# Four look-up chunks compared beside the gate build, first dot products ahead of the pipeline, spill rows moved forward

## The chip, the cores and the metric

The kernel runs on one core of a Trainium2 chip. A core has a matrix engine (TensorE, PE in the rows), a vector engine (VectorE, DVE), a scalar engine (ScalarE, ACT), a general one (GpSimd, POOL) and one that only issues transfers (SyncE, SP). Each takes its instructions in order, and they wait for one another by semaphores. DMA queues of SP, ACT and POOL move data between HBM and the on-chip memory. The metric is the device time of one execution in microseconds, the median of several runs.

## The reference

One encoder layer on 256 tokens of width 2048: a retention and a recurrent branch, cross attention, and a PEER layer, followed by a last norm. Only PEER matters here:

```python
sub_scores = jnp.einsum('thcd,hckd->thck', q, sub_keys)
vals, ids = lax.top_k(sub_scores, PEER_TOPK)
...
top_sc, pos = lax.top_k(cand, PEER_TOPK)
eid = (i1 * PEER_N_KEYS + i2).reshape(t, PEER_HEADS * PEER_TOPK)
gate = jax.nn.softmax(top_sc, axis=-1)
...
u = u_tab[eb]
act = jax.nn.gelu(jnp.einsum('td,tkd->tk', xb, u))
out = jnp.einsum('tk,tkd->td', gb * act, v_tab[eb])
```

Every token chooses 128 of 16384 experts (8 heads, 16 each). An expert is a row of a table `u` and a row of a table `v`, 2048 wide.

## The kernel before

Some experts are chosen by many tokens, others by few. The kernel works the frequent ones densely, as blocks of 128 experts against all 256 tokens, and the others by token: the row of each chosen expert is fetched and multiplied with the token.

*The gate build* (`gbuild`, lines 1105 to 1167; about 1019 to 1165 us) makes, four tokens at a time, the gate of every expert and token (products `G`, L1146) and counts how often each of 88 groups of experts is chosen (`cnt`, L1149). ACT copies `G` into two staging buffers `gs`, the halves `ga` and `gb` (L1152, L1153), and after each of eight groups writes them to memory (L1156 to L1159). `gb` takes turns in three buffers of the tag "ms".

*Dense U blocks* (`u_chunk`, L156) run on PE from before the gate build until 1253 us: five chunks of eight columns, two weight blocks per column, 80 in all. Each block is loaded into `raw` by SP, cast to `hi` by ACT (L135), its rest `lo` taken by DVE (L136), and multiplied as 16 products with `hi` and 8 with `lo`.

*The choice* (`side`, that is `choose` and then `compact`) is woven into these blocks: a list of work is emitted a step at a time between products (`wv.pump`), and a scheduler then orders each engine. `choose` finds the 32 most frequent of the groups and builds `words`, a bit table (L960 to L972; `pow` is a small constant it loads). `compact` looks up, for each of two tiles of 128 tokens, whether each chosen expert is among them: `look_up` takes four chunks per tile, eight in all. A chunk is a 1 MB broadcast load of expert groups (`at_load`, L990, issued by POOL, from `i1d`), a compare in two halves on DVE (L997), 32 small products on PE (L1001, `look<-words`), and two DVE operations on the result (L1005, L1007). Chunks 0, 1, 2, 6 and 7 use h[1] and two pieces `gx`, and 3, 4 and 5 use `at3` to `at5`, three "ms" buffers which the gate build has used last. Then DVE picks the rows to fetch (MAX and MATCH_REPLACE, L935 and L936) and makes their indices; what does not fit into 38 rows per token goes into *spill rows*, whose token (`spti`) and expert (`spi`) are worked out at the end of `compact`.

*The D phase* (1253 to 1495 us) works 32 columns of experts fetched by row (`row<-in_Us_dram`, L1231): PE transposes them (L1372), ACT and DVE split them into `hi` (L1381) and `lo` (L1400), PE multiplies (L145, L147). *V steps* follow until 1903 us with `v`. Both are written out by hand (`run`): each engine keeps the order in which the code emits. Between the steps the generator `chosen` emits, as often as a step's rate allows, one operation for each fetched row: a *dot* with the token (DVE, L1462), a *spill* (a dot of a fetched row with a fetched token, L1542), and in the V steps an *axpy* that adds the row of `v` to the result `hh` (L1470). Rows are fetched by POOL (`fetch`, L1455) into a ring of buffers; a buffer returns when the row behind it was used. Three rows are fetched ahead (`ahead`). Each spill op takes two ring buffers, for the row of `u` and for the token's row of `hn`; they stand behind dot 19 of tile 0 and dot 10 of tile 1. h[0] holds tile 0's tokens (`h`), then tile 1's.

*The end* (`v_final`, from 1903 us) multiplies the last blocks (L1636) on PE while DVE adds the last 12 rows (`closing`) and ACT and DVE form the norm.

## Time and profile before

| | us |
|---|---|
| runs before, median (lowest to highest) of 3 | 1977.03 (1976.32 to 1978.99) |
| profiled execution | 1978.82 |
| its span | 1977.0 |
| look-ups: 1157.5 to 1253.4 | 95.9 |
| D phase: 1253 to 1495 | 242 |
| V steps: 1495 to 1903 | 408 |
| end: 1903 to 1977 | 74 |

The span is the time from the first to the last instruction in one profiled execution; all rows are from it. A row of a timeline has the start, the duration (of the whole group where xN stands), the engine, the line, the operation, the tiles and, in brackets, how long the engine stood idle just before and what ended that wait.

### The profile page before, as it was taken

To read this page: it belongs to the slowest core of one execution; us is meant where nothing else is said; L and a number is where in the kernel's file an instruction comes from. 1 tells how busy PE (TensorE), PEld (TensorE's weight loads), DVE (VectorE), ACT (ScalarE), POOL (GpSimd) and SP (SyncE) were. 2 spreads that over 40 slices of the span, in tenths; PEclk is the share of its full clock that TensorE was granted. 3 is DMA by queue.
4 is the path that set the end of the run, shared out by engine and by line. 5 is a ranking of instruction groups with operands and counts; after the bars stand their busy time and mean duration, and the time that the engine had idled before them with its cause. 6 is when DMAs were issued, how large, how long until landed. Compare 5 with 4: busy or idle time off the path is not lost.

```text
span 1977.0 us, 28501 instructions
## 1 busy us (share of the span) xinstructions
PE 1896.1 (96%) x10644; PEld 1589.4 (80%) x10644; DVE 1500.9 (76%) x2304; ACT 851.6 (43%) x1324; POOL 517.7 (26%) x370
## 2 busy tenths in 40 slices
PE   9999999999999999999999887999989989999997
PEld 8888888888889888899899877988978668656563
DVE  6867968654566656899986667798879889687857
ACT  6566444544455554554456542333334343121111
POOL 0200010000000000000025421355443578477723
PEclk9999999999999999999999988999989999999999
DMA  8775755566664456755557888699898989999993
GB/s 297 260 224 170 208 195 182 154 185 195 185 185 156 149 167 217 251 176 164 186 179 142 166 258 277 235 395 362 321 383 318 383 315 399 379 387 372 421 411 125
DMA packets 203391, 500.97 MB, mean 253 GB/s; under 512 B 106777, under 2 KB 113049, under 8 KB 174873
## 3 DMA queue, kind: packets, MB, share of 16 engines
q1 hardware_dynamic: 72576, 256.33, 39.7%
q0 software_dynamic: 36096, 227.24, 29.5%
q10 hardware_dynamic: 94576, 15.54, 4.8%
q8 instruction: 84, 1.38, 0.3%
q14 instruction: 59, 0.48, 0.1%
HBM read 504.29 MB, written 21.30 MB: 266 GB/s over the span
## 4 chain that ended last, share of the span: by engine, by line
PE 56%; DMA 17%; DVE 14%; issue 9%; POOL 2%; ACT 2%; ACTq 0%; SPq 0%; POOLq 0%; DVEq 0%
PE wb L145 8%; PE xc L198 7%; PE xc L199 7%; PE xc L201 7%; DMA at<-in_Us_dram,idx 6%; PE acc L1213 6%; PE wb L147 4%; PE U L156 4%; DVE lo L136 4%; DMA gt<-gs 3%; DMA at<-in_Vs_dram,idx 2%; DMA kept<-in_V_dram 2%; PE G L1146 2%; PE acc L1194 2%; PE acc L1191 2%
## 5 line engine op out<-in xcount | busy, mean ns | idle before, releaser
L136 DVE TENSOR_TENSOR lo<-raw,hi 128x1024 fp32r<-128x1024 f32 x364 | 448.9, 1235 | 217.3 <-PE xc L201 125.7
L135 ACT CAST hi<-raw 128x1024 fp32r<-128x1024 f32 x364 | 382.1, 1053 | 352.4 <-PE xc L199 173.4
L156 PE MATMUL U<-xn,hi 128*128 128x256 f32 x1280 | 179.9, 292 | 3.8 <-ACT hi L135 3.8
L156 PEld LDWEIGHTS U<-xn,hi 128*128 128x128 f32 x1280 | 167.0, 199 | 4.7 <-ACT hi L135 4.7
L1462 DVE SCALAR_TENSOR_TENSOR junk<-at,h 128x2048 bf16<-128x2048 f32 x64 | 146.2, 2284 | 9.1 <-DMA at<-in_Us_dram,idx 8.9
L1470 DVE SCALAR_TENSOR_TENSOR hh<-at,coef,hh 128x2048 f32<-128x2048 f32 x46 | 108.0, 2348 | 47.3 <-DMA at<-in_Vs_dram,idx 46.7
L145 PE MATMUL U<-xn,hi 128*128 128x512 f32 x512 | 140.2, 407 | 0.0
L794 POOL DMA_DIRECT2D hn<-h x2 | 1.1, 565 | 510.4 <-DVE h L792 510.4
L1383 ACT CAST hi<-kept 128x1024 fp32r<-128x1024 f32 x52 | 53.6, 1051 | 186.9 <-DMA kept<-in_Vs_dram,dyn 127.0
L1455 POOL DMA_INDIRECT at<-in_Us_dram,idx x72 | 86.3, 1199 | 143.4 <-DVE junk L1462 114.4
L145 PE MATMUL wb<-hT,hi 128*128 128x512 f32 x448 | 116.9, 396 | 0.7 <-ACT hi L135 0.7
L1213 PE MATMUL acc<-kept,kept 128*128 128x512 f32 x256 | 110.2, 592 | 0.0
L1133 POOL TENSOR_TENSOR kept<-kept 128x512 f32<-128x512 bf16 x64 | 72.0, 1133 | 130.1 <-DVE kept L1132 90.2
L145 PEld LDWEIGHTS U<-xn,hi 128*128 128x128 f32 x512 | 92.9, 192 | 15.4
L156 PE MATMUL U<-xn,lo 128*128 128x256 f32 x640 | 96.0, 295 | 5.9 <-DVE lo L136 5.5
L1213 PEld LDWEIGHTS acc<-kept,kept 128*128 128x128 f32 x256 | 48.6, 190 | 60.4 <-issue 60.3
L156 PEld LDWEIGHTS U<-xn,lo 128*128 128x128 f32 x640 | 86.5, 201 | 9.2 <-DVE lo L136 8.9
L145 PEld LDWEIGHTS wb<-hT,hi 128*128 128x128 f32 x448 | 80.6, 189 | 14.8 <-ACT hi L135 0.9
L1400 DVE TENSOR_TENSOR lo<-uT,hi 128x512 fp32r<-128x512 f32 x128 | 81.8, 682 | 11.6 <-ACT hi L1381 8.7
L145 PE MATMUL wb<-xT,hi 128*128 128x512 f32 x352 | 90.1, 398 | 0.0
L1132 DVE TENSOR_TENSOR kept<-kept,kept 128x512 bf16<-128x512 bf16 x128 | 63.1, 543 | 32.8 <-PE cnt L1149 23.3
L1455 POOL DMA_INDIRECT at<-in_Vs_dram,idx x46 | 76.0, 1653 | 41.0 <-issue 18.6
(502 smaller groups left out, 4399.3 us busy)
## 6 DMA issues: line engine op xcount, KB each, us to landing
raw<-in_U_dram SPq DMA_DIRECT2D x80, 512.0 KB
raw<-in_w_qkv_dram SPq DMA_DIRECT2D x48, 512.0 KB
raw<-in_w_xyg_dram SPq DMA_DIRECT2D x44, 512.0 KB
raw<-in_V_dram SPq DMA_DIRECT2D x44, 512.0 KB
raw<-in_w_xk_dram SPq DMA_DIRECT2D x32, 512.0 KB
raw<-in_w_xv_dram SPq DMA_DIRECT2D x32, 512.0 KB
raw<-in_w_out_dram SPq DMA_DIRECT2D x32, 512.0 KB
raw<-in_w_xq_dram SPq DMA_DIRECT2D x32, 512.0 KB
```

The costliest lines, as they stand in the source:

```text
L135: A.copy(hi, raw)
L136: V.tensor_tensor(lo, raw, hi.bitcast(F32), op=ALU.subtract)
L145: PE.matmul(pt, hi[:, ks], xt[:, kb, :], start=(kb == 0), stop=(kb == KB - 1))
L156: PE.matmul(pt[:, :T], (lo if part == 2 else hi)[:, k * P:(k + 1) * P], x, start=(part == 0 and kb == 0), stop=(part == 2 and kb == KB - 1))
L198: PE.matmul(pt, xh, hi[:, w], start=(n == 0 and k == 0), stop=False)
L199: PE.matmul(pt, xl, hi[:, w], start=False, stop=False)
L201: PE.matmul(pt, xh, lo[:, w], start=False, stop=(n == 7 and k == 1))
L1213: PE.matmul(acc[dc][tt], av[:, c, tt * P:(tt + 1) * P], row[:, dc * 512:(dc + 1) * 512], start=False, stop=False)
L1400: V.tensor_tensor(los[t][:, s], pts[t][n], his[t][:, s].bitcast(F32), op=ALU.subtract)
L1455: G.indirect_dma_start(dst, None, src, bass.IndirectOffsetOnAxis(ap=ix, axis=0), bounds_check=n - 1, oob_is_err=False)
L1462: V.scalar_tensor_tensor(junk, gat, 1.0, h[0] if rows is None else rows, op0=ALU.mult, op1=ALU.mult, accum_out=coef[tt][:, k:k + 1])
L1470: V.scalar_tensor_tensor(hh[tt], gat, coef[tt][:, k:k + 1], hh[tt], op0=ALU.mult, op1=ALU.add)
```

## The change

The places of the eight look-up chunks are set before the gate build (`places`): h[1], a piece `kept8`, an "ms" buffer `at`, h[0], two pieces of `gx`, then h[1] and `kept8` again. Chunks 0 to 3 are loaded there, and their compares are emitted inside `gbuild` at its steps 20, 30, 40 and 50. The two remaining "ms" buffers hold `gb` in turns. Only chunks 4 to 7 are loaded behind the gate build, 6 and 7 when look-ups 0 and 1 are done. h[0] is reloaded from `hn` by SP behind look-up 3, and the next `hn` load stands behind look-up 5 instead of 3. The first three rows are fetched into `at` and the two `gb` buffers, which then serve as the ring. A loop ahead of the last chunk's gelu emits work until the look-ups are done, since `kept8` holds that chunk's result. The spill tokens are fetched into two `gx` pieces before the D phase, the spill ops stand behind dots 8 and 14 of tile 0 and take one ring buffer each, and three dots are emitted before the hand-written part begins, so that all later dots and axpys come three earlier.

```diff
-SPILL_AT = (19, 10)
+SPILL_AT = (8, 14)
+LOOK_AT = (20, 30, 40, 50)
+EARLY = 3
...
         gates = gbuild()
-        at_load(0)
+        tr["t"] = rp.tile([P, P + 1], F32, tag="cand", name="tri")
+        nc.sync.dma_start(tr["t"], a["tri"])
+        places()
+        for i in range(4):
+            at_load(i)
...
+    def compare(i):
+        at = at_of(i)
+        for n in range(0, 32, 16):
+            V.tensor_scalar(at[:, n:n + 16], at[:, n:n + 16], tr["t"][:, P:], None, op0=ALU.is_equal)
+            yield 0.7
+
+    def places():
+        gbs.extend(slot("ms", [P, P // 2, GT], "gs") for _ in range(2))
+        held = held_in[NCH - 1]
+        ats.extend((h[1], held, slot("ms", [P, D], "at"), h[0], gx["a"], gx["d"], h[1], held))
...
     def look_up(tt):
         for c in range(4):
             at = at_of(4 * tt + c)
-            for n in range(0, 32, 16):
-                V.tensor_scalar(at[:, n:n + 16], at[:, n:n + 16], tr["t"][:, P:], None, op0=ALU.is_equal)
-                yield 0.7
+            if tt:
+                yield from compare(4 * tt + c)
...
-            if 4 * tt + c + len(ats) < 4 * TT:
-                at_load(4 * tt + c + len(ats))
+            if not tt and c < 2:
+                at_load(6 + c)
+            if 4 * tt + c == 3:
+                nc.sync.dma_start(h[0], hn[:P, :])
...
-            if tt and c < 2:
-                ahead.append(fetch(ats[4 + c], a["Us"], NS, idx[0][:, 1 + c:2 + c]))
-            if tt == 0 and c == 3:
+            if 4 * tt + c == 5:
                 nc.sync.dma_start(held_in[NCH + NDY - 1], hn[P:2 * P, :])
...
             if tt == 0:
-                ahead.append(fetch(ats[3], a["Us"], NS, idx[0][:, 0:1]))
+                for n, b in enumerate([ats[2]] + [g.rearrange("p a b -> p (a b)") for g in gbs]):
+                    ahead.append(fetch(b, a["Us"], NS, idx[0][:, n:n + 1]))
...
     def side():
-        ats.extend((gx["a"], gx["d"]))
-        ats.extend(slot("ms", [P, D], f"at{i}") for i in (3, 4, 5))
-        for i in range(1, 6):
+        for i in range(4, 6):
             at_load(i)
...
         for n in range(T // 4 + 1):
+            if n in LOOK_AT:
+                yield from compare(LOOK_AT.index(n))
...
-                    ga, gb = (slot(tag, [P, P // 2, GT], "gs") for tag in ("qs", "ms"))
+                    ga, gb = slot("qs", [P, P // 2, GT], "gs"), gbs[m // (GT // 4) % 2]
...
+            while i == NCH - 1 and not c and "looked" not in done:
+                wv.pump(1.0)
             A.activation(acts[i][:, c, :], pt[:, :T], AF.Gelu_apprx_tanh)
...
     def chosen():
+        spl["x"] = [fetch(gx["bc"[b]], hn, T, spl["ti"][:, b:b + 1]) for b in range(TT)]
...
-                if k == SPILL_AT[tt]:
-                    ops.append(("spill", tt, 0, [(a["Us"], NS, spl["i"][:, tt:tt + 1]), (hn, T, spl["ti"][:, tt:tt + 1])]))
+                if tt == 0 and k in SPILL_AT:
+                    b = SPILL_AT.index(k)
+                    ops.append(("spill", b, 0, [(a["Us"], NS, spl["i"][:, b:b + 1])]))
...
-    wv.add(chosen())
+    row_ops = chosen()
+    for _ in range(EARLY):
+        next(row_ops)
+    wv.add(row_ops)
```

The scheduler moves what is emitted. The compares of chunks 0 to 3 end up on DVE ahead of the whole gate build, where chunk 0's stood before. On PE, all four look-ups of the first tile now follow one another, and behind look-up 5 stand the products of blocks 64 and 65 with `hi` and `lo`, half of look-up 6, the products of blocks 66, 67 and 68 with `hi` alone, the rest of look-up 6 and half of 7, and only then those of 66 with `lo`. On SP, before: the load of `pow`, one `raw`, one `hn`, then 12 `raw`; now: `pow`, one `raw`, two `hn`, then 13 `raw`, each with the waits of its buffer.

Three places on DVE follow. Line numbers of the changed kernel are its own (there L138 is the `lo` of L136, L1023 and L1025 the two steps on a look-up of L1005 and L1007, L1030 to L1034 the steps of L1014 to L1018, L941 the pick of L935, L1481 the dot of L1462, L1419 the `lo` of L1400). The first place is just ahead of the picks of the first token tile; before:

```order
L136 TENSOR_TENSOR lo_11426<-raw_11423,hi_11425 128x1024
L1014 CAST kept1_7764<-kept1_7764 128x128
L1005 TENSOR_TENSOR kept1_7764<-look_11343,kept2_7765 128x352
L1015 TENSOR_TENSOR kept1_7764<-kept1_7764,kept2_7765 128x128
L136 TENSOR_TENSOR lo_11494<-raw_11491,hi_11493 128x1024
L1016 TENSOR_SCALAR kept1_7764<-kept1_7764 128x128
L136 TENSOR_TENSOR lo_11574<-raw_11571,hi_11573 128x1024
L1018 TENSOR_TENSOR key_8575<-key_8575,kept1_7764 128x128
L1018 TENSOR_TENSOR work_8576<-work_8576,kept1_7764 128x128
L935 MAX sel_11195<-key_8575 128x8
```

and in the changed kernel (h1 holds chunk 6 there):

```order
L1025 TENSOR_REDUCE kept1_7764<-kept1_7764 128x32
L997 TENSOR_SCALAR h1_4236<-h1_4236,tri_9497 128x2048
L1030 CAST kept1_7764<-kept1_7764 128x128
L138 TENSOR_TENSOR lo_11314<-raw_11311,hi_11313 128x1024
L1031 TENSOR_TENSOR kept1_7764<-kept1_7764,kept2_7765 128x128
L1023 TENSOR_TENSOR kept1_7764<-look_11341,kept2_7765 128x352
L1032 TENSOR_SCALAR kept1_7764<-kept1_7764 128x128
L138 TENSOR_TENSOR lo_11419<-raw_11416,hi_11418 128x1024
L1034 TENSOR_TENSOR key_8575<-key_8575,kept1_7764 128x128
L1034 TENSOR_TENSOR work_8576<-work_8576,kept1_7764 128x128
L941 MAX sel_11187<-key_8575 128x8
```

Three `lo` blocks stood ahead of the picks, now there are two, and the first half of chunk 6's compare stands ahead of both. The second place is behind these picks, where the two tiles' work meets; before (kept0 holds chunk 7):

```order
L950 SCALAR_TENSOR_TENSOR sel2_11196<-sel_11195,sel2_11196 128x56
L1005 TENSOR_TENSOR kept1_7764<-look_11455,kept2_7765 128x352
L997 TENSOR_SCALAR kept0_7763<-kept0_7763,tri_10949 128x2048
L1007 TENSOR_REDUCE kept1_7764<-kept1_7764 128x32
L136 TENSOR_TENSOR lo_11624<-raw_11621,hi_11623 128x1024
L1005 TENSOR_TENSOR kept1_7764<-look_11522,kept2_7765 128x352
L136 TENSOR_TENSOR lo_11682<-raw_11679,hi_11681 128x1024
L1007 TENSOR_REDUCE kept1_7764<-kept1_7764 128x32
L136 TENSOR_TENSOR lo_11736<-raw_11733,hi_11735 128x1024
L1014 CAST kept1_7764<-kept1_7764 128x128
L136 TENSOR_TENSOR lo_11801<-raw_11798,hi_11800 128x1024
L1015 TENSOR_TENSOR kept1_7764<-kept1_7764,kept2_7765 128x128
```

and in the changed kernel (kept8 holds chunk 7):

```order
L956 SCALAR_TENSOR_TENSOR sel2_11188<-sel_11187,sel2_11188 128x56
L997 TENSOR_SCALAR kept8_7771<-kept8_7771,tri_9497 128x2048
L138 TENSOR_TENSOR lo_11487<-raw_11484,hi_11486 128x1024
L997 TENSOR_SCALAR kept8_7771<-kept8_7771,tri_9497 128x2048
L138 TENSOR_TENSOR lo_11567<-raw_11564,hi_11566 128x1024
L1023 TENSOR_TENSOR kept1_7764<-look_11515,kept2_7765 128x352
L138 TENSOR_TENSOR lo_11617<-raw_11614,hi_11616 128x1024
L1025 TENSOR_REDUCE kept1_7764<-kept1_7764 128x32
L138 TENSOR_TENSOR lo_11675<-raw_11672,hi_11674 128x1024
L1030 CAST kept1_7764<-kept1_7764 128x128
L138 TENSOR_TENSOR lo_11729<-raw_11726,hi_11728 128x1024
L1031 TENSOR_TENSOR kept1_7764<-kept1_7764,kept2_7765 128x128
```

Four `lo` blocks are seen there before and five now; ahead of this piece the compare of at5 is gone, and the blocks that follow are lower in number by two. The third place is the start of the D phase; before:

```order
L136 TENSOR_TENSOR lo_12079<-raw_12076,hi_12078 128x1024
L1083 TENSOR_SCALAR spt_11724<-spt_11724 128x1
L1088 SCALAR_TENSOR_TENSOR j1_11787,w1_11784<-iota_79,w1_11784,ls_11779 128x18
L1090 CAST spi_11726<-w1_11784 128x1
L1091 SCALAR_TENSOR_TENSOR j1_11787,spg_11727<-iota_79,w1_11784,ls_11779 128x18
L1400 TENSOR_TENSOR lo_12184<-uT_12135,hi_12175 128x512
L1400 TENSOR_TENSOR lo_12184<-uT_12136,hi_12175 128x512
L1400 TENSOR_TENSOR lo_12187<-uT_12145,hi_12178 128x512
L1400 TENSOR_TENSOR lo_12187<-uT_12146,hi_12178 128x512
L1400 TENSOR_TENSOR lo_12203<-uT_12155,hi_12181 128x512
L1400 TENSOR_TENSOR lo_12203<-uT_12156,hi_12181 128x512
L1462 SCALAR_TENSOR_TENSOR junk_12117,coef_12226<-at3_10951,h0_4235 128x2048
```

and in the changed kernel:

```order
L1481 SCALAR_TENSOR_TENSOR junk_12110,coef_12117<-at_9501,h0_4235 128x2048
L138 TENSOR_TENSOR lo_12042<-raw_12039,hi_12041 128x1024
L138 TENSOR_TENSOR lo_12072<-raw_12069,hi_12071 128x1024
L1481 SCALAR_TENSOR_TENSOR junk_12110,coef_12117<-gs_9499,h0_4235 128x2048
L1481 SCALAR_TENSOR_TENSOR junk_12110,coef_12117<-gs_9500,h0_4235 128x2048
L1419 TENSOR_TENSOR lo_12194<-uT_12145,hi_12185 128x512
L1419 TENSOR_TENSOR lo_12194<-uT_12146,hi_12185 128x512
L1419 TENSOR_TENSOR lo_12197<-uT_12155,hi_12188 128x512
L1419 TENSOR_TENSOR lo_12197<-uT_12156,hi_12188 128x512
L1419 TENSOR_TENSOR lo_12213<-uT_12165,hi_12191 128x512
L1419 TENSOR_TENSOR lo_12213<-uT_12166,hi_12191 128x512
L1481 SCALAR_TENSOR_TENSOR junk_12110,coef_12117<-at_9501,h0_4235 128x2048
```

One dot now stands ahead of the last two `lo` blocks of U and two more ahead of the first `lo` of the D phase, where before there was none until its sixth row.

More of the change, by code (lines that the diff above doesn't have):

```diff
@@ L981, in chosen_rows @@
         yield 0.8
-    ats = []
+    ats, gbs = [], []
     def at_of(i):
-        return ats[i % len(ats)].bitcast(BF16).rearrange("p (s t) -> p s t", t=P)
+        return ats[i].bitcast(BF16).rearrange("p (s t) -> p s t", t=P)
+    def compare(i):
[7 more added lines that the diff above has]
+        ats.extend((h[1], held, slot("ms", [P, D], "at"), h[0], gx["a"], gx["d"], h[1], held))
     def at_load(i):
         tt, c = divmod(i, 4)
-        G.dma_start(ats[i % 6].bitcast(BF16), i1d[tt, 32 * c:32 * c + 32].rearrange("s t -> (s t)")[None, :].to_broadcast([P, 32 * P]))
+        G.dma_start(ats[i].bitcast(BF16), i1d[tt, 32 * c:32 * c + 32].rearrange("s t -> (s t)")[None, :].to_broadcast([P, 32 * P]))
     def look_up(tt):
@@ L1025, in compact @@
             yield from look_up(tt)
+            if tt:
+                done.add("looked")
             if not tt:
@@ L1098, in side @@
     def side():
-        tr["t"] = rp.tile([P, P + 1], F32, tag="cand", name="tri")
-        nc.sync.dma_start(tr["t"], a["tri"])
         wv.rate = RK
-        ats.extend((gx["a"], gx["d"]))
-        ats.extend(slot("ms", [P, D], f"at{i}") for i in (3, 4, 5))
-        for i in range(1, 6):
+        for i in range(4, 6):
             at_load(i)
@@ L1519, in chosen @@
             elif kind == "spill":
-                spill_dot(tt, mine[0], mine[1])
+                assert NCH + 1 + tt not in acts
+                spill_dot(tt, mine[0], spl["x"][tt])
             elif kind == "axpy":
@@ L1721, in hybrid_layer_kernel @@
     gx.update(zip("abcd", kept))
-    ats.append(h[1])
     for tt in range(TT):
```

## The prediction

> **What bounds the kernel now.** I read the page first, then the busy table by stretches, then the timelines of TensorE (PE), VectorE (DVE) and GpSimd (POOL) in the stretch that is not full.
>
> ```profile
> PE 1896.1 (96%) x10644; PEld 1589.4 (80%) x10644; DVE 1500.9 (76%) x2304; ACT 851.6 (43%) x1324; POOL 517.7 (26%) x370
> PE   9999999999999999999999887999989989999997
> ```
>
> PE is busy 96% of the span; only its holes can be won. A slice is 49.4 us long; those that are not 9 lie at 1087 to 1236 us (end of the gate build and the look-ups), at 1433 to 1483 (in the D phase), at 1581 to 1631 (V steps, where the change moves little) and at the end.
>
> Columns below: the stretch, its length, then busy time with instruction count for PE, weight loads, DVE, ACT and POOL; granted clock, DMA share, GB/s.
>
> ```profile
> 1157.50:1253.40 95.90, 75.73 (x756) 73.28 (x753) 61.50 (x223) 23.85 (x37) 13.32 (x14) 0.88 0.74 243
> 1240.00:1253.40 13.40, 12.93 (x110) 12.72 (x108) 4.14 (x20) 2.90 (x6) 0.00 (x0) 1.00 0.01 4
> ```
>
> The look-up stretch lasts 95.9 us and PE is idle for 20.2 of them. Its last part shows PE at full clock: 110 instructions in 12.93 us, 0.118 us each, so one weight block (16 products with hi, 8 with lo) costs 2.8 us. These are PE's larger holes and DVE's and POOL's behind them:
>
> ```profile
> 1162.13 2.60 PE L1146 MATMUL G<-kept,kept 128*128 128x128 f32 x16 [3.10 <-POOL kept L1133]
> 1173.98 1.00 PE L1001 MATMUL look<-words,h 128*128 128x11 bf16 x32 [3.38 <-DVE words L972]
> 1205.75 0.59 PE L1001 MATMUL look<-words,at 128*128 128x11 bf16 x16 [8.05 <-DVE at L997]
> 1221.33 3.50 PE L156 MATMUL U<-xn,hi 128*128 128x256 f32 x16 [2.36 <-ACT hi L135]
> ...
> 1167.90 0.75 DVE L997 TENSOR_SCALAR at<-at,tri 128x2048 bf16<-128x2048 bf16 x1 [7.63 <-DMA at<-i1d]
> 1172.50 0.31 DVE L970 SCALAR_TENSOR_TENSOR kept<-kept,best,kept 128x88 f32<-128x88 f32 x1 [0.50 <-DMA kept<-in_pow_dram]
> 1204.93 0.75 DVE L997 TENSOR_SCALAR at<-at,tri 128x2048 bf16<-128x2048 bf16 x1 [8.34 <-DMA at<-i1d]
> ...
> 1160.42 0.58 POOL L990 DMA_DIRECT2D at<-i1d  x1 [5.15 <-DVE best L965]
> 1199.85 0.53 POOL L990 DMA_DIRECT2D at<-i1d  x1 [19.09 <-DMA gt<-gs]
> ...
> 1166.18 33.13 DMA gt<-gs
> ```
>
> The reader is to see one chain: the last gate write (issued 1166.18, landed 33.13 us later) holds the buffer of at5, POOL waits 19.09 us for it, the load lands at 1204.93, DVE's compare and PE's look-up stand still until then. Before that, the chain from the counts to `words` stands 7.63 us behind the compare of at4, and POOL's own load at 1160.42 keeps PE 3.10 us from its last gate products.
>
> **The change part by part.** *Look-ups.* Chunks 0 to 3 are loaded and compared ahead of the gate build, and chunks 4 to 7 go to buffers that no gate write holds. So 3.10 us on PE, 7.63 and 8.34 us on DVE go. What is late next is DVE's own order, as the rows of the order show: the compare of chunk 6 stands ahead of the first token tile's picks, behind it only two lo blocks (64 and 65) come ahead of the picks, where before there were three (to 67), and blocks 66 to 71 come only after them. Working it forward:
>
> ```profile
> 1175.27 0.53 POOL L990 DMA_DIRECT2D h<-i1d  x1 [9.69 <-PE look L1001]
> 1182.10 0.75 DVE L997 TENSOR_SCALAR h<-h,tri 128x2048 bf16<-128x2048 bf16 x1
> 1188.99 0.29 DVE L935 MAX8 sel<-key 128x8 f32<-128x128 f32 x1
> 1195.35 0.29 DVE L1035 MAX8 m<-key 128x8 f32<-128x128 f32 x1
> L136 DVE TENSOR_TENSOR lo<-raw,hi 128x1024 fp32r<-128x1024 f32 x364 | 448.9, 1235 | 217.3 <-PE xc L201 125.7
> ```
>
> The first look-up waited for `words` until 1173.98; the three rounds ahead of that need no data but the small pow load, which is issued when the last gate product is done (3.1 us earlier), so I take 1170. Four look-ups follow (1.0 us each by the row at 1173.98), and DVE's eight steps on them with four half compares of 0.75 us end near 1178.5. Chunk 6 is issued after look-up 0, at 1171.5; the same load took at most 6.8 us above (1175.27 to 1182.10, and DVE did not idle for it) and 7.5 in the at4 case (1160.42 to 1167.90), so it is there at 1179: DVE loses 0 to 1 us, and I take 0.5. The Trainium skill, "DMA: Bandwidth & Descriptors", section "Anatomy of one DMA — SWDGE (gpsimd) path", fits such a load by 2.0 us plus its bytes over 436 GB/s, an estimate of 4.4 us for this 1 MB; by that the compare would wait for nothing, and the sum below would be 17.5 instead of 17. The rows above, 6.8 and 7.5 us with other queues busy, do not agree with it here.
>
> Two lo blocks (1.24 us each) and the small steps put the picks at 1184; they last 6.4 us (1188.99 to 1195.35), some 4 us of index steps and compares follow, so the third lo block comes at 1196. PE has by then done its blocks up to 65 of the 80 and the hi halves of 66 to 68 (ending near 1191), so it waits about 5 us there, where before it waited 8.05. From 1196 it runs with DVE: six lo blocks until 1207, the second tile's picks, the next lo block at 1215.5 (PE waits 4 us), and then 7.6 blocks of 2.8 us, 21.3 us, until 1237. I add 3 us for products at a reduced clock after the two waits (16 took 3.50 us at 1221.33, and 1.9 by the full-clock row: 1.6 each) and 2.3 for the dot product that now stands ahead of two lo blocks: 1242. Two more dots of 2.3 us hold the D phase's first lo block until about 1246; in before it came at 1254.75:
>
> ```profile
> 1253.39 3.71 PE L1372 MATMUL uT<-ident,row 128*128 128x128 f32 x32 [0.47 <-ACT kept L1179]
> 1254.75 3.68 DVE L1400 TENSOR_TENSOR lo<-uT,hi 128x512 fp32r<-128x512 f32 x6 [8.66 <-ACT hi L1381]
> ```
>
> **Gain 9 us.** Bounds: if PE's two new waits (5 and 4 us) come out double, 9 us more, so 0; if the picks begin at once and PE never waits, 16. On the queues:
>
> ```profile
> L990 POOL DMA_DIRECT2D at<-i1d x3: 530/583/586, 1146.5 to 1199.8; - x3
> L990 POOL DMA_DIRECT2D kept<-i1d x3: 542/575/581, 1163.4 to 1180.2; - x3
> L990 POOL DMA_DIRECT2D h<-i1d x2: 530/532/535, 954.2 to 1175.3; - x2
> 1185.52 50.88 SPq L128 DMA_DIRECT2D raw<-in_U_dram  x12
> ```
>
> seven of these eight loads were issued from 1146.5 on, and now it is four; SP one more (h[0], 1 MB, after look-up 3) ahead of 13 weight loads; those stand behind look-up 5, near 1178.5, where before they stood behind look-up 3 until 1185.5. The two extra rows of hn are issued when the DMA share is 0.01 (the row of 1240 above): nothing.
>
> *Compares ahead of the gate build.* Six halves more on DVE near 1000:
>
> ```profile
> 950.00:1015.00 65.00, 61.36 (x500) 60.13 (x500) 64.59 (x158) 31.06 (x41) 3.92 (x4) 1.00 0.63 194
> 1015.00:1157.00 142.00, 131.13 (x1143) 128.57 (x1143) 94.58 (x154) 85.75 (x205) 67.12 (x60) 0.96 0.77 163
> L997 DVE TENSOR_SCALAR h<-h,tri x4: 744/746/748, 1000.3 to 1183.2; 128x2048 bf16<-128x2048 bf16 x4
> ```
>
> 6 x 0.75 = 4.5 us on an engine that is full there (64.59 of 65). What follows is the gate build, where DVE is busy 94.58 of 142 us, and PE has blocks of U to go on with. I take **0.5 us lost**; without that cover 4.5.
>
> *Two buffers for the gate's second half instead of three.* The first copy of a group now waits for the write of the group two before.
>
> ```profile
> 1106.93 3.19 ACTq L1159 DMA_DIRECT2D gt<-gs  x1
> 1128.73 0.37 ACT L1153 COPY gs<-G 128x256 f32<-128x256 f32 x1
> ...
> 1142.44 17.28 DMA gt<-gs
> ```
>
> Such a copy comes 21.8 us after the write's issue, and a write landed after 17.28: 4.5 us to spare, cost 0. Behind a late one on ACT stand the next hi casts and the copies that free G, so PE would wait too. Bound: the 33.13 of the last write, 11.3 us for each of six groups.
>
> *D phase.* Spill rows need one ring buffer instead of two, their hn rows are there beforehand, and three dots are already done.
>
> ```profile
> PE uT L1372 <- DVE lo L1400: 12.7, 6, 4.3
> DVE junk L1542 <- DMA at<-hn,spti: 9.8, 2, 5.2
> ...
> 1346.06 1.31 PE L1372 MATMUL uT<-ident,row 128*128 128x128 f32 x8 [3.25 <-DVE lo L1400]
> 1475.73 1.97 PE L1372 MATMUL uT<-ident,h 128*128 128x128 f32 x8 [4.32 <-DVE lo L1400]
> L1462 DVE SCALAR_TENSOR_TENSOR junk<-at,h 128x2048 bf16<-128x2048 f32 x64 | 146.2, 2284 | 9.1 <-DMA at<-in_Us_dram,idx 8.9
> ```
>
> 3.25 and 4.32 are behind the two spill dots; the other 5.1 of 12.7 I leave as they are. Of the 7.6 I take **6**, since a spill's row still takes a place in the ring; bounds 0 and 10.
>
> *Tail.* All dots and axpys run three ahead, so the two axpys left over behind the last step go ahead of it, and the fetches of the closing rows start earlier.
>
> ```profile
> 1901.81 4.74 DVE L1470 SCALAR_TENSOR_TENSOR hh<-at,coef,hh 128x2048 f32<-128x2048 f32 x2
> 1922.25 2.35 DVE L1470 SCALAR_TENSOR_TENSOR hh<-at,coef,hh 128x2048 f32<-128x2048 f32 x1 [15.70 <-DMA at<-in_Vs_dram,idx]
> 1964.02 1.02 PE L1674 MATMUL acc<-h,oh 128*128 128x512 f32 x2
> 1967.98 0.68 DVE L1675 TENSOR_TENSOR hh<-hh,acc 128x512 f32<-128x512 f32 x1
> ```
>
> DVE can save 4.74 and much of 15.70, but PE ends at 1965.04 either way, 2.9 us ahead of DVE's last sum: **2.5 gained**, bounds 0 and 2.9.
>
> **Sum:** 9 - 0.5 + 6 + 2.5 = 17. The profiled execution took 1978.8 us (span 1977.0); 1978.8 - 17 = 1961.8. The median of the runs is 1.8 below the profiled one, so I forecast **1960**.
>
> **Rivals.** (1) *Raw loads late.* SP's 13 loads stand behind look-up 5 and 2 MB of hn, and by the program's waits the fourth of them behind the last gate write. If that write lands at 1199 again and the loads follow as the one that ended in the wait at 1221.33, PE waits some 6 us more and the D phase gives 4: 9 us gained, 1968. For it: DMA share 0.74 over the stretch. Against: three of the seven loads are gone from there. (2) *No wait is left.* DVE's picks start on time, bound 16 in the look-ups, 8 in the D phase, 2.9: 27, so 1950. For it: DVE's 16 us of idle in the rows above. Against: the lo blocks behind the picks. (3) *Slower: the gate writes.* If a write lands later than 21.8 us after its issue, each of six groups stalls ACT by the rest; at 26 us, 25 us in all, against 17 gained: 1985. It ends slower than before by 4 us from (17 + 4) / 6 = 3.5 us each, a landing of 25.3. For it: 33.13 us for the last write. Against: that one ran beside the late at-loads, the one before it with one of them took 17.28, and the four loads now made earlier are issued long before the first write. The Trainium skill, "DMA: Bandwidth & Descriptors", section "Queues, rings and completion order", has each DMA engine take turns, packet by packet, between the queues that have work; by that a write of many small packets gets slower only with more queues at work beside it, 17.28 and 33.13 agree with it, and this rival's chance would be 0.03 and not 0.06. (4) *It doesn't do what it says:* the wait of at5 becomes one for chunks 6 and 7 with the lo blocks behind it, the new waits eat the old ones, and only the tail is left: 2.5, 1974.5.
>
> **How the numbers follow.** Forecast (1953 to 1967) 0.50; raw loads late (1967 to 1973) 0.18; no wait left (1946 to 1953) 0.17; no net effect 0.09; slower 0.06. What a measurement of this kernel can tell from no change is about 0.2%, 4 us. Faster by more than that: 0.50 + 0.18 + 0.17 = 0.85; within: 0.09; slower: 0.06. The range 1948 to 1973 holds the forecast, rival 1 and most of rival 2, and takes in the bounds of the look-ups (0 to 16) one at a time.
>
> **What would show it.** In the new profile: no wait of POOL for gt<-gs and none of DVE for the at-loads above 2 us; a wait of PE for a lo block near 1191 to 1196 and one near 1211 to 1215; the D phase's first lo block at about 1246; the waits of PE behind the spill dots gone; the last sum of DVE within 0.5 us of PE's end. It is wrong if ACT waits for gt<-gs inside the gate build, if PE waits for raw loads after look-up 5, or if the D phase shows as many waits under other names.

## The result and the profile after

The changed kernel takes **1965.24 us** (median of 5 runs, 1961.5 to 1968.87), beside 1976.32 us of the kernel before on the same chip (5 runs, 1972.35 to 1978.99): a ratio of 0.9943, with a 95% interval of 0.9925 to 0.9961, or 11.1 us gained. The forecast was 1960, in a range of 1948 to 1973. The profiled execution took 1966.72 us, its span is 1964.9 (1977.0 before).

To see where the 12.1 us of the spans come from, five points are taken that every kernel of this study has: a `lo` product of U near 948 us, ahead of all that was changed; the first transpose of the D phase; the first product of the V steps; the first product of the end; DVE's last sum. They cut the stages a little later than the table ahead of the prediction does. In the timelines of the kernel before (the rows at 1253.39 and 1967.98 stand in the prediction):

```profile
949.81 1.21 PE L156 MATMUL U<-xn,lo 128*128 128x256 f32 x8 [0.19 <-DVE lo L136]
1507.79 0.40 PE L1191 MATMUL acc<-hi,a 128*128 128x512 f32 x1
1903.06 9.20 PE L1636 MATMUL acc<-last,kept 128*128 128x512 f32 x21
```

and of the changed one:

```profile
947.57 1.22 PE L158 MATMUL U<-xn,lo 128*128 128x256 f32 x8 [0.19 <-DVE lo L138]
...
1251.68 3.71 PE L1391 MATMUL uT<-ident,row 128*128 128x128 f32 x32 [0.47 <-ACT kept L1198]
...
1498.09 0.40 PE L1210 MATMUL acc<-hi,a 128*128 128x512 f32 x1
...
1893.95 13.89 PE L1658 MATMUL acc<-last,kept 128*128 128x512 f32 x32
...
1954.89 1.02 PE L1696 MATMUL acc<-at,oh 128*128 128x512 f32 x2
...
1955.95 0.69 DVE L1697 TENSOR_TENSOR hh<-hh,acc 128x512 f32<-128x512 f32 x1 [2.41 <-PE acc L1696]
```

The first column, the start, is what is read. By differences, before and after: up to the common point 949.8 and 947.6 (nothing is changed there, so two executions differ by that much by themselves); from there to the D phase 303.6 and 304.1; D phase 254.4 and 246.4; V steps 395.3 and 395.9; end 64.9 and 62.0. **The D phase and the end gave what was forecast or more, the look-ups nothing.**

That is not because the look-ups did not move. PE's timeline of the changed kernel between the gate build and the D phase, its larger holes:

```profile
1161.22 0.94 PE L1017 MATMUL look<-words,h 128*128 128x11 bf16 x32 [0.30 <-DVE best L984]
...
1182.58 3.79 PE L158 MATMUL U<-xn,hi 128*128 128x256 f32 x16 [12.05 <-ACT hi L137]
...
1196.51 2.18 PE L158 MATMUL U<-xn,hi 128*128 128x256 f32 x16 [1.44 <-ACT hi L137]
1201.91 0.59 PE L1017 MATMUL look<-words,kept 128*128 128x11 bf16 x16 [2.83 <-DVE kept L997]
1213.04 2.17 PE L158 MATMUL U<-xn,hi 128*128 128x256 f32 x16 [1.48 <-ACT hi L137]
1224.24 0.50 PE L158 MATMUL U<-xn,lo 128*128 128x256 f32 x2 [2.19 <-DVE lo L138]
```

The first look-up starts 213.7 us behind the common point, where before it was 224.2 (1173.98 - 949.81): 10.5 us ahead. Of that, 6.0 us is idle time of PE up to there (20.99 us before, 14.95 now), the waits of 3.10 and 3.38 us among it; the other 4.5 us is work that PE now does behind that look-up (1716 instructions ahead of it before, 1703 now). Then PE stands still for 12.05 us, for a `hi` of ACT; before, its longest wait for a `hi` in that stretch was 2.36 us. ACT's timeline, its waits and its queue's issues (ACTq) there:

```profile
1157.16 1.47 ACTq L1175 DMA_DIRECT2D gt<-gs  x1
1158.73 22.43 ACTq L1176 DMA_DIRECT2D gt<-gs  x1
1181.21 0.38 ACT L1198 ACTIVATE kept<-U 128x256 f32<-128x256 f32 x1 [24.21 <-DMA gt<-gs]
```

ACT's next instruction, a gelu, starts as the second of these rows ends (1158.73 + 22.43 = 1181.16, the gelu at 1181.21), and its input was ready long before: in late_write below, without the write there, it runs at 1161.41. So the issue itself held ACT for 22.43 us, and the gelu and the next four `hi` casts stand behind it. Before, the same write held it half as long; the rows that group the eight writes (min/median/max in ns), of before:

```profile
L1159 ACTq DMA_DIRECT2D gt<-gs x8: 3165/3188/10804, 1034.7 to 1166.2; - x8
```

and of the changed kernel:

```profile
L1176 ACTq DMA_DIRECT2D gt<-gs x8: 2946/3182/22435, 1032.7 to 1158.7; - x8
```

The other seven are as they were (3.17 to 3.83 us before, 2.95 to 3.94 now), and ACT waits for no gate write ahead of the last one, so two buffers in place of three cost nothing. Beside the last one, POOL's timeline has the loads of chunks 4 to 7 all within 7 us of it, and SP's the two loads of `hn`, 1 MB each:

```profile
1156.78 1.11 POOL L1007 DMA_DIRECT2D kept<-i1d  x2 [2.18 <-ACT gs L1169]
1162.46 0.53 POOL L1007 DMA_DIRECT2D h<-i1d  x1 [4.57 <-PE look L1017]
1163.26 0.53 POOL L1007 DMA_DIRECT2D kept<-i1d  x1 [0.27 <-PE look L1017]
...
1165.01 0.33 SPq L1021 DMA_DIRECT2D h<-hn  x1
1170.56 0.33 SPq L1027 DMA_DIRECT2D kept<-hn  x1
```

Before, POOL had issued three of its loads in the 6 us ahead of this write (1166.18): the one at 1160.42 that the prediction shows, and

```profile
1163.37 0.58 POOL L990 DMA_DIRECT2D kept<-i1d  x1 [0.30 <-POOL kept L1133]
1165.04 0.54 POOL L990 DMA_DIRECT2D kept<-i1d  x1 [1.09 <-PE G L1146]
```

The next came 9.1 us behind it, at 1175.27, and `hn` only at 1180.31. So what is new is behind the start of the write: in the first 12 us two chunks and both loads of `hn`, where before there was one chunk.

### The profile page after: what moved, and what is told of

Read it like the earlier page. It is cut to its first block, busy times and chain, and to the rows that moved or that the text cites. A ratio compares the mean times of both kernels' runs of the same rounds, so it can differ in the third digit from the quotient of the medians.

```text
span 1964.9 us, 28497 instructions
## 1 busy us (share of the span) xinstructions
PE 1888.0 (96%) x10644; PEld 1584.1 (81%) x10644; DVE 1499.5 (76%) x2304; ACT 850.5 (43%) x1324; POOL 526.3 (27%) x370
## 4 chain that ended last, share of the span: by engine, by line
PE 62%; DMA 16%; DVE 9%; issue 7%; POOL 3%; ACTq 1%; ACT 1%; POOLq 0%; SPq 0%; DVEq 0%
PE wb L147 11%; PE xc L200 7%; PE xc L201 7%; PE xc L203 7%; PE U L158 7%; PE wb L149 6%; DMA gs<-in_Us_dram,idx 3%; DMA at<-in_Us_dram,idx 3%; PE acc L1658 3%; PE acc L1232 3%; DMA h<-in_Vs_dram,idx 2%; DVE lo L138 2%; PE G L1163 2%; DMA kept<-gt,dyn 2%; DMA raw<-in_V_dram 1%
## 5 line engine op out<-in xcount | busy, mean ns | idle before, releaser
L138 DVE TENSOR_TENSOR lo<-raw,hi 128x1024 fp32r<-128x1024 f32 x364 | 448.7, 1234 | 222.2 <-PE xc L203 122.6
L1489 DVE SCALAR_TENSOR_TENSOR hh<-gs,coef,hh 128x2048 f32<-128x2048 f32 x32 | 75.2, 2349 | 40.9 <-DMA gs<-in_Vs_dram,idx 40.5
L1481 DVE SCALAR_TENSOR_TENSOR junk<-gs,h 128x2048 bf16<-128x2048 f32 x43 | 98.2, 2285 | 8.8 <-DMA gs<-in_Us_dram,idx 8.8
L1419 DVE TENSOR_TENSOR lo<-uT,hi 128x512 fp32r<-128x512 f32 x128 | 81.8, 681 | 7.3 <-ACT hi L1400 7.1
L1474 POOL DMA_INDIRECT gs<-in_Us_dram,idx x49 | 56.8, 1160 | 101.3 <-DVE junk L1481 91.1
L200 PE MATMUL xc<-hi,xT 128*128 128x512 f32 x192 | 76.3, 398 | 0.0
```

What stands on the lines that cost most here:

```text
L138: V.tensor_tensor(lo, raw, hi.bitcast(F32), op=ALU.subtract)
L200: PE.matmul(pt, xh, hi[:, w], start=(n == 0 and k == 0), stop=False)
L1419: V.tensor_tensor(los[t][:, s], pts[t][n], his[t][:, s].bitcast(F32), op=ALU.subtract)
L1481: V.scalar_tensor_tensor(junk, gat, 1.0, h[0] if rows is None else rows, op0=ALU.mult, op1=ALU.mult, accum_out=coef[tt][:, k:k + 1])
L1489: V.scalar_tensor_tensor(hh[tt], gat, coef[tt][:, k:k + 1], hh[tt], op0=ALU.mult, op1=ALU.add)
```

## The experiments

In the table each kernel's stages are worked out from its own profiled execution, as above, and the median, the ratio to the kernel before and its interval are from the timed runs. The V steps are the same work in all of them and differ by up to 6.5 us between executions (392.7 to 399.2), so a stage of one execution shows what is larger than a few us, and the ratios have to carry the rest. The scheduler also orders every kernel anew. hn_late and chunks_late keep the changed kernel's order on PE between the look-ups and the D phase; write_sp, late_write, late_both and chunks_held do not, and old_late_write does not keep that of d_part. What these five show in the first stage is the moved transfer together with the new order.

| kernel | to the D phase | D | V | end | median us | ratio, 95% interval |
|---|---|---|---|---|---|---|
| before | 303.6 | 254.4 | 395.3 | 64.9 | 1976.32 | |
| changed | 304.1 | 246.4 | 395.9 | 62.0 | 1965.24 | 0.9943 (0.9925 to 0.9961) |
| d_part | 302.4 | 247.0 | 392.7 | 62.0 | 1963.52 | 0.9923 (0.9900 to 0.9946) |
| look_part | 303.9 | 256.3 | 396.6 | 63.6 | 1978.55 | 1.0008 (0.9992 to 1.0024) |
| write_sp | 302.7 | 249.5 | 399.2 | 62.0 | 1967.42 | 0.9949 (0.9933 to 0.9965) |
| hn_late | 297.8 | 249.1 | 397.3 | 62.0 | 1963.62 | 0.9921 (0.9896 to 0.9947) |
| spill_only | 303.4 | 248.5 | 393.8 | 64.8 | 1970.07 | 0.9965 (0.9953 to 0.9977) |
| early_only | 303.5 | 251.9 | 395.8 | 62.0 | 1974.69 | 0.9982 (0.9968 to 0.9996) |
| late_write | 293.7 | 246.2 | 399.0 | 62.0 | 1953.78 | 0.9878 (0.9857 to 0.9900) |
| late_both | 291.5 | 244.9 | 395.3 | 62.0 | 1950.43 | 0.9870 (0.9844 to 0.9895) |
| chunks_late | 302.9 | 246.6 | 394.7 | 62.0 | 1964.23 | 0.9938 (0.9919 to 0.9958) |
| chunks_held | 296.9 | 248.8 | 395.0 | 62.0 | 1960.86 | 0.9911 (0.9875 to 0.9946) |
| old_late_write | 292.6 | 252.9 | 398.0 | 62.0 | 1960.62 | 0.9914 (0.9898 to 0.9931) |

**The change in two halves.** *d_part* is the kernel before with the spills and the early dots alone:

```diff
-SPILL_AT = (19, 10)
+SPILL_AT = (8, 14)
+EARLY = 3
+        spl["x"] = [fetch(gx["bc"[b]], hn, T, spl["ti"][:, b:b + 1]) for b in range(TT)]
```

> Before, with only the part of the change that lies behind the look-ups: spill tokens fetched ahead, spill ops at dots 8 and 14, three dots early. Theory (the look-up part brings next to nothing, since ACT was held 22.43 us by the issue of the last gate write): this part alone keeps its 6.1 us in the D phase and 2.9 us at the end, so 8 to 10 us faster than before, about 1967, with the look-up stretch as long as before. Rival (the look-ups earn most, and the D phase is faster only because it starts earlier): under 5 us, over 1971.

*look_part* is the changed kernel without them:

```diff
-SPILL_AT = (8, 14)
-EARLY = 3
+SPILL_AT = (19, 10)
+EARLY = 0
```

> After, with only the look-up part: spill ops at 19 and 10 with two ring buffers, no early dots. Theory: the look-ups alone give 0 to 4 us (1972 to 1977), with the waits behind the spill dots and the tail as before, and the long issue on ACT (about 22 us) and PE's wait of about 12 us for hi in place. Rival: 6 us or more, under 1970.

The first half is worth 12.6 us (1976.14 of the kernel before, run beside it, less 1963.52), the second nothing: by its interval between 1.6 us gained and 4.7 lost. By medians 12.6 less 2.4, 10.2 us, beside 11.1 of the whole change: within their intervals the halves add up. look_part has ACT's long issue too, and PE's wait behind it:

```profile
1158.76 22.65 ACTq L1177 DMA_DIRECT2D gt<-gs  x1
...
1182.83 3.79 PE L159 MATMUL U<-xn,hi 128*128 128x256 f32 x16 [11.29 <-ACT hi L138]
```

**Is it ACT that is held, or the transfers?** *write_sp* gives the last write to SP's queue:

```diff
-                    A.dma_start(rows[:, P // 2 - RD:, ts], gb)
+                    (A if m < T // 4 - 1 else nc.sync).dma_start(rows[:, P // 2 - RD:, ts], gb)
```

> After, with the last of the eight large gate writes issued by SP instead of ACT; same bytes. Theory (ACT's issue is what holds the casts): the casts of blocks 64 to 67 come at about 1163 to 1168, PE's wait of 12.05 us for hi goes or falls below 4, the look-up stretch ends 5 to 9 us earlier, 1956 to 1960. SP's loads then stand behind that issue, so some of it may come back as waits for raw. Rival 1 (DVE's picks ahead of lo block 66 are the limit anyway): PE's wait moves to lo 66, under 3 us gained, over 1962. Rival 2 (weight loads late): the waits for raw grow by what the other wait shrinks, 1965.

ACT cast at once (at 1160.57), but SP's queue was held in its place, by the issue behind the write, and the raw loads behind that came late:

```profile
1157.81 0.39 SPq L1176 DMA_DIRECT2D gt<-gs  x1
1165.39 16.23 SPq L1021 DMA_DIRECT2D h<-hn  x1
1181.73 0.85 SPq L130 DMA_DIRECT2D raw<-in_U_dram  x2
...
1191.81 0.80 PE L158 MATMUL U<-xn,hi 128*128 128x256 f32 x2 [14.25 <-ACT hi L137]
1204.29 3.59 PE L158 MATMUL U<-xn,hi 128*128 128x256 f32 x16 [6.99 <-ACT hi L137]
```

Moving the issue alone gains nothing (0.9949 beside 0.9943), and the 1956 to 1960 us of the theory did not come: SP's queue pays for that write as ACT's did. *hn_late* takes 2 MB from beside it: both loads of `hn` wait for look-up 7.

```diff
-            if 4 * tt + c == 3:
-                nc.sync.dma_start(h[0], hn[:P, :])
...
-            if 4 * tt + c == 5:
-                nc.sync.dma_start(held_in[NCH + NDY - 1], hn[P:2 * P, :])
+            if 4 * tt + c == 7:
+                for n, b in enumerate((h[0], held_in[NCH + NDY - 1])):
+                    V.tensor_copy(b[:, :1], fl[:, 127:])
+                    nc.sync.dma_start(b, hn[n * P:n * P + P, :])
```

> After, with both 1 MB loads of hn held until look-up 7, so that 2 of the about 6 MB that are moved beside the last gate write go. Theory (the issue lasts as long as the write's small packets wait in the shared DMA engines): the issue shrinks from 22.4 to 13 to 17 us and PE's wait for hi from 12 to 4 to 8; 1958 to 1962. Rival (the issue's length is the write's own): 22 us again, no gain, 1964 to 1967.

```profile
1158.10 17.89 ACTq L1176 DMA_DIRECT2D gt<-gs  x1
...
1177.41 3.78 PE L158 MATMUL U<-xn,hi 128*128 128x256 f32 x16 [6.51 <-ACT hi L137]
```

The issue falls to 17.89 us (13 to 17 were expected), PE's wait behind it from 12.05 to 6.51, and the stretch by 6.3 us. In both kernels PE starts again 1.42 us after the issue ends (1175.99 here, 1181.16 there), with the same order on PE: the length of the issue is what it waits for. By time hn_late can't be told from the changed kernel (the intervals overlap).

**The write out of the way.** *late_write* issues the last write only when the first tile's four look-ups are done:

```diff
-                    A.dma_start(rows[:, P // 2 - RD:, ts], gb)
+                    if m < T // 4 - 1:
+                        A.dma_start(rows[:, P // 2 - RD:, ts], gb)
+                    else:
+                        held_write.append((rows[:, P // 2 - RD:, ts], gb))
...
+        if not tt:
+            dst, gb = held_write[0]
...
+            V.tensor_scalar(zero, fu[:, :1], 0, None, op0=ALU.bitwise_and)
...
+            V.tensor_tensor(one, one, zero, op=ALU.bitwise_or)
+            A.dma_start(dst, gb)
```

> The changed kernel, with the last write of the gate's second half issued by ACT only when the first tile's four look-ups are done (a real dependency; in the changed kernel it stands at 1158.7, its issue takes 22.43 us, and the casts of blocks 64 to 68 stand behind it). Theory A: ACT, held 22 us in that issue, is what eats the gain of the look-ups. Then the casts of 64 to 68 run near 1160, PE's wait of 12.05 us for hi falls below 4, the stretch up to the D phase gets 4 to 9 us shorter than 304.1, and the time is 1956 to 1961. Rival B: what is scarce is the transfers, and whatever stands behind the write waits; the issue then holds ACT a few us later, raw loads come late, PE waits as long under another name, and the time stays at 1963 to 1970.

> The same late write, and also both hn loads (2 MB) held until look-up 7. Theory A: the casts are free and the write then has less beside it, its issue takes at most 12 us, the stretch up to the D phase is 294 to 299 us long (297.8 with the hn loads held alone), and the time is 1953 to 1960. Rival B, the transfers are scarce in any order: the stretch is no shorter than 298 and the time is 1962 or more.

late_write: 1953.78 us, better than the 1956 to 1961 expected, and the stretch is 10.4 us shorter than the changed kernel's: 7.0 us of it is idle time of PE, and 3.4 us is that PE was busy for 263.60 us with the same 2399 instructions, where it had been 266.95. In its timelines of ACT and PE, the first rows and the largest holes that are left:

```profile
1161.69 2.93 ACT L137 CAST hi<-raw 128x1024 fp32r<-128x1024 f32 x3
...
1182.03 5.17 ACTq L1041 DMA_DIRECT2D gt<-gs  x1
1187.92 6.47 ACTq L1066 DMA_DIRECT2D spare_keys<-key  x1
...
1190.57 0.59 PE L1017 MATMUL look<-words,kept 128*128 128x11 bf16 x16 [6.34 <-DVE kept L997]
1196.39 3.35 PE L158 MATMUL U<-xn,hi 128*128 128x256 f32 x14 [5.23 <-ACT hi L137]
```

Three casts run 20 us before they did and the wait of 12.05 us is gone; two smaller ones come behind it. The one of 6.34 us is for a compare that stands on DVE behind the first tile's picks, which last until 1188; the other is for a `hi` behind the write's new place. late_both, the same with `hn` held, has the best time of all, 1950.43; the write's issue takes 0.37 us there and the stretch is 291.5. The two can't be told apart by their intervals.

**What holds the issue?** *chunks_late* moved the loads of chunks 4 and 5 behind look-ups 0 and 1 in the code:

```diff
-        for i in range(4, 6):
-            at_load(i)
...
-            if not tt and c < 2:
-                at_load(6 + c)
+            if not tt:
+                at_load(4 + c)
```

> The changed kernel, with chunks 4 to 7 loaded by POOL behind look-ups 0 to 3, so that none of them (before: two, 2 MB of broadcast, issued at 1156.8) stands ahead of the last gate write. The write keeps its place on ACT. Theory A: the length of its issue goes with what other queues have given the DMA engines just ahead of it; the issue falls from 22.43 us to 12 or less, PE's wait for hi of 12.05 us falls below 5, and the time is 1955 to 1962 unless the later chunks give it back. Rival B: the issue is held by the two gate writes ahead of it on ACT's own queue (their landing), not by the loads; it stays at 17 us or more, and the time is 1964 or more.

It tells nothing: the two buffers are free, so the loads were issued at 1157.21 all the same, ahead of the write. The kernel is the changed one over again, and gives the same (22.33 us in the issue, 12.06 on PE, 1964.23). *chunks_held* really holds all four, by a number of look-up 3 that is put into each buffer first:

```diff
-            if not tt and c < 2:
-                at_load(6 + c)
...
+            if not tt and c == 3:
+                for i in range(4, 8):
+                    V.tensor_copy(ats[i][:, :1], fl[:, 127:])
+                    at_load(i)
...
-        for i in range(4, 6):
-            at_load(i)
```

> The changed kernel, with chunks 4 to 7 really held: each one's buffer is first touched by DVE with a number from look-up 3 (near 1170), so that none of the four 1 MB loads is issued ahead of the last gate write or in the first 10 us beside it. Theory A, traffic of other queues holds the issue: it falls from 22.4 us to 14 or less, PE's wait for hi of 12.05 us falls below 6; the second tile's look-ups come later, and the time is 1956 to 1964. Rival B, ACT's own queue holds it: 19 us or more in the issue, PE's wait stays above 9, and the time is 1964 or more.

Its timelines of ACT, POOL and PE:

```profile
1158.63 4.25 ACTq L1176 DMA_DIRECT2D gt<-gs  x1
...
1163.20 3.88 ACT L137 CAST hi<-raw 128x1024 fp32r<-128x1024 f32 x4
1175.34 23.80 ACTq L1061 DMA_DIRECT2D spare_keys<-key  x1
...
1168.08 1.13 POOL L1007 DMA_DIRECT2D kept<-i1d  x2 [1.38 <-DVE kept L1032]
...
1180.53 0.59 PE L1017 MATMUL look<-words,kept 128*128 128x11 bf16 x16 [8.36 <-DVE kept L997]
...
1201.04 3.78 PE L158 MATMUL U<-xn,hi 128*128 128x256 f32 x16 [5.42 <-ACT hi L137]
```

The same write, in the same place behind the same two writes, is issued in 4.25 us when the chunk loads come behind it. Rival B falls: it is the loads, not ACT's own queue alone. But the write isn't gone by then: the next issue on ACT, 64 KB, behind four loads, took 23.80 us, PE waits 5.42 behind that, and 8.36 for a chunk that comes later. So the stretch gains 7.2 us, not the 10.4 of late_write; by time alone chunks_held can't be told from the changed kernel.

**Does the late write need the change?** *old_late_write* puts it into d_part, with the old order of the look-ups; chunk 5 uses the write's buffer there, so its load stands behind the write.

```diff
+            A.dma_start(dst, gb)
+            ats.append(slot("ms", [P, D], "at5"))
+            at_load(5)
...
-        for i in range(1, 6):
+        for i in range(1, 5):
```

> The kernel before with the spill and early-dot part only (1963.5 us measured), and the late write added: the last gate write is issued after the first tile's look-ups, and chunk 5, whose buffer it reads from, is loaded behind it. Theory A: the late write is worth what it is only because the change took the gate's buffers away from the chunks; here at5 comes still later, PE's wait for it (9 us) grows past 15, and the time is 1966 to 1980. Rival B: the free ACT is all that counts, and the time is 1953 to 1961, as in the changed kernel with the late write.

Theory A fell. The compare of at5 moves to 1211.37, but DVE waits only 0.86 us for the load and PE not at all, since the scheduler puts U blocks ahead of it:

```profile
1212.17 0.56 PE L1003 MATMUL look<-words,at 128*128 128x11 bf16 x16
```

The stretch is 292.6, as short as with the look-ups moved (293.7). How much of that is the write's new place and how much the new order on PE, this run does not part. Part of it is given back in the D phase, 252.9 against 247.0 of d_part, where PE waits 11.2 us for `lo` instead of 6.5; the time, 1960.62, can't be told from d_part.

**The first half in its parts.** *spill_only* has EARLY = 0, *early_only* the old spills (behind dots 19 and 10) and EARLY = 3.

> The kernel before, with the spill tokens fetched ahead and the spill ops behind dots 8 and 14 of tile 0, but without the three early dots. Theory A: the two long waits of PE behind the spill dots (3.25 and 4.32 us) are what the spill part removes; waits of PE for lo in the D phase fall from 12.7 to 5 to 8 us, the end stays as before (PE 2.9 us ahead of the last sum), and the time is 1968 to 1972, 5 to 8 us under before. Rival B: the earlier dots empty the D phase, and the spills only move their waits: waits stay above 10 and the time is within 3 us of before.

> The kernel before, with three dots emitted ahead of the hand-written part and the spills as they were (behind dots 19 and 10, two ring buffers each). Theory A: only the end gains, 2 to 3 us (64.9 to 62.0), the D phase keeps 10 us or more of waits for lo, and the time is 1972 to 1975. Rival B: the early dots empty the D phase as well (247 instead of 254 us), and the time is 1964 to 1969.

Both times came as theory A had them: 7.0 and 2.4 us gained, with intervals of 4.5 to 9.3 and 0.8 to 6.3, which leave room for the 12.6 of both. spill_only's D phase is 6.0 us shorter with the end as before (64.8), and PE's waits for `lo` there are 8.2 us, where 5 to 8 were expected; early_only has its end at 62.0 and keeps 10.8 us of waits in the D phase. The D-phase waits of PE (us, times, longest), of the changed kernel, against 12.7 before:

```profile
PE uT L1391 <- DVE lo L1419: 6.6, 4, 4.8
```

and of early_only:

```profile
PE uT L1373 <- DVE lo L1401: 10.8, 10, 3.4
```

## Why the prediction was right in its range and wrong in its first term

- **Look-ups, 9 us forecast: about 0 measured.** The first part of the working held and more: `words` came 10.5 us earlier against the common point, where I had 4 (1170 for 1173.98), no wait of POOL for the gate write is left, and DVE's largest wait for a chunk fell from 8.34 us to 2.61. (One reading of mine was short: POOL's load at 1160.42, which kept PE waiting for 3.10 us, most likely waited for a gate write as well. The row names DVE, but in d_part, with the same code there, POOL waits 6.65 us for `DMA gt<-gs` ahead of that load.) The step that failed is the price of the last gate write. I took it by its landing and by the buffer that it holds, and put the time for which its issue holds ACT, with the casts behind it, at nothing; the row of 10804 ns was there to be seen. It came to 22.43 us on ACT and 12.05 on PE. The sentence "seven of these eight loads were issued from 1146.5 on, and now it is four" counts the loads and does not ask which of them meet that write. That the loads make the hold is shown by chunks_held (4.25 us with the four chunks behind it) and hn_late (17.89 without `hn`); the share of each is not. late_write gives what the stretch can gain without it, 10.4 us, its new order on PE included.
- DVE's order, from which I had taken waits of 5 and 4 us on PE, was hidden behind that hold. In the changed kernel 2.83 us for a compare at 1201.91 and 2.19 for a `lo` at 1224.24 are left of it (1.44 and 1.48 us at 1196.51 and 1213.04 are for `hi`, behind raw loads). Where ACT is free it shows: 6.34 us for the compare behind the picks in late_write, and 2.85, 3.04 and 3.60 us for a compare and two `lo` in late_both.
- So the change took away a form of the wait. In the old order the last gate write cost PE by its *landing* (at5's buffer, 8.05 us on PE), in the new one by its *issue* (12.05 us). Put behind the burst, neither wait is there: 302.4 to 292.6 us with the old order of the look-ups, 304.1 to 293.7 with the new. With the write in either place the two orders are equal up to the D phase, within what one execution can show. That the cause is one and the same in both is argued from these numbers; the kernels with the late write also have a new order on PE.
- **Rival 1, late raw loads,** was partly there: ACT waited for raw loads in that stretch, 6.41 us at the most (just ahead of PE's 1.48 at 1213.04), and write_sp shows what it is in full. Its 1968 is close to the time, its place isn't the main one.
- **Rival 3, late gate writes,** named the right instruction and the wrong one of the eight: the issue of none of the first seven got slower than 3.94 us. The DMA view of the changed kernel from 1150 to 1200 us (queue, packets, MB, share of 16 engines) shows what runs beside the last; q10 is ACT's queue, q0 POOL's:

```profile
q0 software_dynamic: 969, 7.15, 36.0%
q10 hardware_dynamic: 13073, 2.10, 24.8%
```

On average a packet of ACT's queue has 2.10 MB / 13073 = 161 bytes, one of POOL's 7.4 kB. The Trainium skill, "DMA: Bandwidth & Descriptors", section "Queues, rings and completion order", has each DMA engine take turns between the queues packet by packet; by that each small packet waits for a large one, and 22.43 us with the loads beside the write against 4.25 with the chunks held fit it. No run here shows the turns themselves, and the sizes alone do not make the difference: the same view of the kernel before has 153 bytes and 7.3 kB, with a hold of 10.80 us. The forecast took from this rule that rival 3 was less likely; it bears just as much on the last write, which I did not ask.
- **Compares ahead of the gate build, 0.5 us lost; buffers, 0:** neither shows. The first look-up is 10.5 us ahead, and the seven writes' issues are unchanged.
- **D phase, 6 us forecast: 8.0** in the changed kernel, 7.4 in d_part. The spills alone give 6.0, as worked out from the two waits of 3.25 and 4.32 us. The columns of the prediction's tables, for the D phase before and now:

```profile
1253.40:1507.80 254.40, 241.50 (x1537) 215.27 (x1538) 223.04 (x288) 94.88 (x204) 124.50 (x89) 0.98 0.91 350
1251.70:1498.10 246.40, 239.59 (x1537) 214.01 (x1538) 222.58 (x286) 92.09 (x201) 120.21 (x88) 0.99 0.93 360
```

PE's idle time fell from 12.9 to 6.8 us, by the 6 that were forecast; the other 1.9 us is that the same 1537 instructions took less. The spill dots now wait 0.31 us at the most for a row; a wait of 4.79 us that is left, at 1424.30, stands behind the dot of an ordinary row that came late.
- **Tail, 2.5 us forecast: 2.9.** DVE's last sum starts at 1955.95, when PE's last product ends (1954.89 + 1.02); before, it came 2.9 us behind it. early_only, with the end at 62.0, and spill_only, with 64.8, show that it is the early dots.
- In sum 8.0 and 2.9 gained and 0.5 lost, 10.4 us; with 0.6 lost in the V steps and 2.2 gained ahead of all changes it is 12.0 of the 12.1 between the spans. The range held because the large miss was at the lower bound that the look-ups had been given (0 to 16), and the D phase and the end came out 2.4 us higher. For the look-ups that is luck: their bound of 0 was worked out from waits of PE behind DVE coming out double, not from an issue that holds ACT. For the D phase and the end the mechanism was right and not only the number.
- Of the signs named, the last sum of DVE and the waits behind the spill dots came as said. DVE still waits 2.61 us for a chunk, where 2 was the limit, and the first `lo` of the D phase starts at 1253.05 and not near 1246.

## What to carry to other kernels

- A transfer has three prices: its landing, its buffer, and the time for which its issue holds the engine. The third is read from the maximum, not the median, of the issue's row, and it lands on whatever stands behind the issue on that engine, here the casts that feed TensorE.
- When loads are moved out of the way, count what is in flight beside the transfers that stay, by the time at which it is issued, not only the loads that are left. A write that nobody waits for soon can go behind the burst (late_write: 1953.78 against 1965.24 us).
- A load that is written later in the code is not issued later unless something real holds it: in chunks_late two of them were issued at 1157.21 all the same.
- When an experiment lets a scheduler order the kernel anew, compare the order too, or the gain has two causes (late_write, old_late_write).

## What the runs showed that was not expected

The issue of a gate write of 1 MB on ACT took 2.95 to 3.94 us for the first seven of eight, before and in the changed kernel, and for the last one 8.43 to 18.95 us in four kernels with the old order (spill_only, d_part, before, early_only: 8.43, 8.91, 10.80, 18.95) and 22.33 to 22.65 in three with the new. The hold passes on along the queue: SP issued the write in 0.39 us and was then held 16.23 by the transfer behind it, and in chunks_held 4.25 us for the write were followed by 23.80 for one of 64 KB. Whether the issue waits for room in the queue or for something else these records don't show. It stays open, too, what makes the hold of the old order differ by a factor of two between executions of the same instructions there, and why its stretch stays at 303.4 to 303.6 us with 8.43, 10.80 and 18.95 alike.
